# PEER block: nops between scattered adds, scatters paced in blocks of nine, four first-product banks, and 24 instead of 32 tokens by gathered rows

## The chip, the core and the metric

One core of a Trainium2 chip runs the whole kernel as one program. The time is device microseconds of one execution, the median of several; the engines are TensorE (PE; its weight loads are PEld), VectorE (DVE), ScalarE (ACT), GpSimd (POOL) and the DMA queues of SyncE (SP), ACT and POOL.

## The reference

One decoder layer over 512 tokens of width 1024 in float32: a projection, gated linear attention, sliding-window attention, an output projection, and then PEER, a layer of 16384 single-neuron experts. Only PEER is touched:

```
best, pos = lax.top_k(cand, 16)                  # 8 heads x 16 experts for each token
idx  = take_along_axis(cand_idx, pos);  gate = softmax(best)
u = expert_u[idx];  h = gelu(einsum('lkd,ld->lk', u, x))
out = einsum('lk,lkd->ld', gate * h, expert_v[idx])
```

A token needs 128 rows of U and of V, and the 512 tokens together need nearly all experts.

## The kernel before

The kernel computes PEER in two ways at once. For most tokens (TD = 352, columns TG = 160 to 511) it is **dense**: all 128 blocks of 128 experts are multiplied with all those tokens, and a matrix of gates (g, mostly zeros) picks what counts. For the first 160 tokens rows are **gathered**.

*Dense.* A first product (h_step, "U block") multiplies one block of U with the tokens: 24 matmuls of 352 columns (L202; 8 pieces of the width, three products of split float32 each), then ACT applies Gelu (L1334) into a ring, of which most is spilled to DRAM (hs) and loaded back later. A second product (v_step, "V block") multiplies gate times h (wr, w_a; split into wh and wl) with a block of V: again 24 matmuls (L1384), into eight banks that stay open for a phase. There are three phases: 92 U blocks and 92 V blocks, 20 and 20, 16 and 16; called U1, V1, U2, V2, U3, V3 here. Every block's weights (512 KB) come through SP's queue (raw), ACT rounds them (whi, L141) and DVE takes the difference (wlo, L151). The first products write to two PSUM banks in turn (M0, M1).

*The gates.* For tokens 160 to 383 (56 groups of four) DVE builds one-hot matrices (oh), PE multiplies them (gp, L1154, between the matmuls of U blocks), ACT copies them to gbuild, and SP writes them to DRAM (gd). For tokens 384 to 511 the gates (w3) are added into a zeroed DRAM array (g3) by 128 scatters on POOL, L1110, one for each pair of head and rank; a tiny store (memset of gap, L1109) stands ahead of each. Inside a head's 16 scatters no order is asked for; the first of a head waits until all of the head before have landed (after, L1120). Before each U block's pump some scatters are written into POOL's stream, so that all are out by block 88. The first V block needs gd, all of g3 and so the last head's landing: g_load loads both into gt, 32 times in all, the first two at block 89.

*Gathered rows.* The first 128 tokens, one per partition, take 128 row gathers on POOL (L1268, 1 MB each: U row and V row of one expert for each partition); tokens 128 to 159 are put four times beside each other (XR = 4 copies of XG = 32), which takes 32 more. For each, DVE multiplies U with x and sums (L1304), ACT makes the gated Gelu (L1305, L1306, tile misc), and DVE adds the V row (L1288). While the gates are being built ("early") these rows lie in two buffers named row; later in two pairs named rows.

*Order.* All engines run their own stream in program order. What stands where is planned while the program is written: pump() keeps running sums of what PE, DVE, POOL and the DMA queue would have used (pe, dve, pool, dma) and puts a step of the gather in when none is ahead of PE by more than SLACK; an early row is used three pumps after its issue at the earliest. What the planner did not fit in is done at once (flush, behind block 122 and so ahead of the last five blocks of V3).

Of the kernel before, what the change touches and what calls it, by code (L numbers as in the profile page):

```python
# [23 lines left out]
KB = 8  # L24
# [22 lines left out]
NRP = 11  # L47
# [6 lines left out]
GL = 3  # L54
XG = 32
# [6 lines left out]
CT = 32  # L62
NCK = TD // CT
NSC = 128 // CT
NGR = (TD - 128) // 4
CQ = CT // 4

# [6 lines left out]
def tile_block(ctx, tc, xT, wst, smalls, wgk2, keysT, uT, vv, uv_rows, out):  # L74
# [934 lines left out]
    gd = DR.tile([NB // 4, 128, NCK - NSC, 4 * CT], F32, name="gd")  # L1009
# [42 lines left out]
    def decode(t):  # L1052
        ij = R.tile([128, 2, 128], F32, name="ij", tag="ij", bufs=2)
        for sd in range(2):
            eq = eq_mult(t, sd)
            yield
            yield from tree(ij[:, sd], eq)
        gf = gate[:, t].rearrange("p h k -> p k h")
        if t == 0:
            nc.vector.scalar_tensor_tensor(eidx, ij[:, 0], 128.0, ij[:, 1], OP.mult, OP.add)  # L1060
            nc.vector.tensor_copy(wgt.rearrange("p (k h) -> p k h", h=8), gf)
            return
        if t == 3:
            nc.vector.tensor_copy(w3.rearrange("p (k h) -> p k h", h=8), gf)
            place(ij)
            return
        gk = R.tile([128, 128], F32, name="gkh", tag="gkh")
        nc.vector.tensor_copy(gk.rearrange("p (k h) -> p k h", h=8), gf)
        if t == 1:
            e1 = R.tile([128, 128], I32, name="e1")  # L1070
            nc.vector.scalar_tensor_tensor(e1, ij[:, 0], 128.0, ij[:, 1], OP.mult, OP.add)
            for r in range(XR):
                rs, n = slice(r * XG, (r + 1) * XG), min(XS, 128 - r * XS)
                nc.sync.dma_start(eid2[rs, 0:n], e1[0:XG, r * XS:r * XS + n])
                nc.sync.dma_start(wgt2[rs, 0:n], gk[0:XG, r * XS:r * XS + n])
# [10 lines left out]
    gap = XP.tile([1, 1], F32, name="gap")  # L1086
# [3 lines left out]
    def place(ij):  # L1090
        r4 = R.tile([128, 128], I32, name="r4")
        tk = R.tile([128, 4], I32, name="tk")
        nc.gpsimd.iota(tk[:, 0:1], pattern=[[0, 1]], base=0, channel_multiplier=1)
        nc.vector.tensor_scalar(tk[:, 1:2], tk[:, 0:1], 96, None, OP.bitwise_and)
# [10 lines left out]
        nc.vector.scalar_tensor_tensor(addr, f, 32.0 - 16384.0, a, OP.mult, OP.add)  # L1105

    def scatter(h, k):
        c = k * 8 + h
        nc.gpsimd.memset(gap, 0.0)  # L1109
# [8 lines left out]
        pool[0] += 2.1  # L1118
# [26 lines left out]
    def gmm(n):  # L1145
# [3 lines left out]
        if q == 0:  # L1149
            gbs[c] = Dn.tile([128, 128, CT], F32, name="gbuild", tag="gbuf", bufs=2)  # L1150
# [5 lines left out]
        if q == CQ - 1:  # L1156
            g = gbs.pop(c).rearrange("p (q i) t -> p q (i t)", i=4)

            def put(x):
                nc.sync.dma_start(gd[x:x + 4, :, c].rearrange("q j x -> j q x"), g[:, x:x + 4])  # L1160
                xfer(0.9)

            gout.extend([lambda x=x: put(x) for x in range(0, 32, 4)])

    def route():
# [76 lines left out]
    nc.gpsimd.memset(misc[:, 384:384 + 2 * XS], 0.0)  # L1242

    def gather():
# [8 lines left out]
        def issue(k):  # L1255
            nonlocal grp, n
            while n < min(n_, k + (3 if late[0] else 2)):
                for i in range(min(2 if late[0] else 1, n_ - n)):
# [19 lines left out]
        for k in range(n_ + 1):  # L1278
            if k:
                kind, s_ = slots[k - 1]  # L1280
# [19 lines left out]
            if k < n_:  # L1300
# [4 lines left out]
                nc.scalar.activation(hc, hc, AF.Gelu)  # L1305
                nc.scalar.activation(hc, hc, AF.Copy, scale=w_[0:m, s_:s_ + 1])  # L1306
# [8 lines left out]
    later = []  # L1315
# [87 lines left out]
    per = NGR / (N0 - LEAD - TAIL - 3) / KB  # L1403
    due = [0.0]

    def feed():
        due[0] += per
        while due[0] >= 1:
            due[0] -= 1
            next(r_, None)  # L1410


    def pump():
        for x in (dve, dma, pool):
            x[0] = max(x[0], pe[0] - SLACK)
        turn[0] += 1
# [46 lines left out]
    BANKS = ("S2", "S2", "PT", "O", "M2", "M3", "M0", "M1")  # L1463
    for ph, (b0, b1) in enumerate(PHASES):
        for b in range(b0, b1):
# [4 lines left out]
            h_step(b, feed if LEAD <= b < N0 - TAIL - 3 else None)  # L1470
# [144 lines left out]
```

## Time and profile before

| | |
|---|---|
| runs | 1807.66 us median of 3 (1807.25 to 1811.36) |
| profiled execution | 1808.49 us, its span 1806.6 us |
| busy share of PE, DVE, ACT, POOL | 94%, 73%, 42%, 43% |
| moved by DMA | 436.69 MB, 242 GB/s over the span |
| mean granted TensorE clock | 0.974 of full |

The busy shares are means over stages that have different limits: from 0 to 665 us the kernel computes attention, the projections and the routing scores; from 665 us the dense PEER runs. A stage is read from its own window, and a stall from the row of the engine that waits and of the one that released it.

### The profile page before, as it was taken

The page shows a single profiled execution, that of the slowest core. Times are in us where ns is not written, and L with a number is a line of the kernel's source. Part 1 is how long each engine was busy: PE and PEld are TensorE (multiplying, and loading weights), DVE is VectorE, ACT ScalarE, POOL GpSimd, SP SyncE. Part 2 cuts the span into 40 slices and gives each one's busy share as a digit, 9 for nine tenths or more (in the row PEclk, how much of TensorE's full clock was granted, in tenths as well). Part 3 has the DMA queues.
Part 4 walks back from the last instruction along what each step waited for, and adds up shares of the span by engine and source line. Part 5 has one row for each costly group of instructions (what it writes and reads, how often), then busy time and mean ns, then how long its engine had stood idle before and what let it go on. Part 6 is the DMA issues. An engine that isn't in the chain of part 4 may idle for free.

```text
span 1806.6 us, 26403 instructions
## 1 busy us (share of the span) xinstructions
PE 1690.4 (94%) x9812; PEld 1558.2 (86%) x9812; DVE 1321.8 (73%) x2491; ACT 760.0 (42%) x1360; POOL 782.1 (43%) x601
## 2 busy tenths in 40 slices
PE   7899999999997999999899897999999999999974
PEld 5676688987886889999899897999999999999973
DVE  7647714346246997996777754898898988998986
ACT  5445523335244234454454443444444444444431
POOL 3333444444544451788877782222221332332230
PEclk9999999999998999999999998999999999999986
DMA  4223442222243234699899999999999999998984
GB/s 158 79 70 94 145 136 81 70 82 71 93 143 136 84 107 140 195 271 274 261 281 283 276 288 331 377 402 403 404 394 402 381 357 385 378 402 354 373 339 172
DMA packets 161521, 436.69 MB, mean 242 GB/s; under 512 B 30720, under 2 KB 76160, under 8 KB 140528
## 3 DMA queue, kind: packets, MB, share of 16 engines
q1 hardware_dynamic: 114880, 254.53, 40.5%
q0 software_dynamic: 41472, 167.86, 26.2%
q10 hardware_dynamic: 5040, 12.62, 1.9%
q8 instruction: 77, 1.26, 0.3%
q14 instruction: 52, 0.43, 0.1%
HBM read 394.45 MB, written 40.47 MB: 241 GB/s over the span
## 4 chain that ended last, share of the span: by engine, by line
PE 61%; DVE 14%; DMA 11%; issue 5%; ACT 4%; POOL 3%; SPq 1%; POOLq 0%; DVEq 0%; ACTq 0%
PE mm L202 17%; PE oa L1384 16%; PE hp L202 13%; PE oacc L1384 5%; DMA rows<-in_uv_rows_dram,misc 5%; PE mm L219 4%; DVE wlo L151 2%; POOL g L1110 2%; DMA raw<-in_uT_dram 1%; DMA row<-in_uv_rows_dram,misc 1%; DVE accv L1288 1%; PE gp L1154 1%; DMA g<-w,addr 1%; ACT whi L141 1%; DMA gd<-gbuild 1%
## 5 line engine op out<-in xcount | busy, mean ns | idle before, releaser
L141 ACT CAST whi<-raw 128x1024 fp32r<-128x1024 f32 x349 | 362.9, 1043 | 129.1 <-DMA raw<-in_vv_dram 30.1
L1268 POOL DMA_INDIRECT rows<-in_uv_rows_dram,misc x128 | 187.9, 1468 | 490.1 <-DVE accv L1288 374.4
L202 PE MATMUL hp<-xh,whi 128*128 128x352 f32 x1024 | 340.3, 332 | 35.4 <-ACT hw L1334 29.2
L151 POOL TENSOR_TENSOR wlo<-raw,whi 128x1024 fp32r<-128x1024 f32 x99 | 244.5, 2474 | 240.2 <-ACT whi L141 235.3
L202 PE MATMUL hp<-xh,wlo 128*128 128x352 f32 x1024 | 334.6, 327 | 0.0
L202 PE MATMUL hp<-xl,whi 128*128 128x352 f32 x1024 | 333.2, 325 | 0.0
L151 DVE TENSOR_TENSOR wlo<-raw,whi 128x1024 fp32r<-128x1024 f32 x250 | 304.9, 1221 | 37.7 <-ACT whi L141 16.1
L1110 POOL DMA_INDIRECT g<-w,addr x128 | 246.1, 1922 | 102.3 <-issue 37.7
L1384 PE MATMUL oa<-wh,wlo 128*128 128x352 f32 x768 | 249.8, 325 | 33.0 <-DVE wlo L151 33.0
L1384 PE MATMUL oa<-wh,whi 128*128 128x352 f32 x768 | 249.6, 325 | 0.0
L1384 PE MATMUL oa<-wl,whi 128*128 128x352 f32 x768 | 249.5, 325 | 0.0
L202 PEld LDWEIGHTS hp<-xh,whi 128*128 128x128 f32 x1024 | 196.4, 192 | 39.5 <-ACT hw L1334 32.2
L202 PEld LDWEIGHTS hp<-xl,whi 128*128 128x128 f32 x1024 | 196.4, 192 | 0.0
L202 PEld LDWEIGHTS hp<-xh,wlo 128*128 128x128 f32 x1024 | 195.9, 191 | 0.0
L1305 ACT ACTIVATE misc<-misc 128x1 f32<-128x1 f32 x160 | 32.5, 203 | 353.1 <-DVE rows L1304 235.7
L1384 PEld LDWEIGHTS oa<-wh,wlo 128*128 128x128 f32 x768 | 145.8, 190 | 33.5 <-DVE wlo L151 33.5
L1384 PEld LDWEIGHTS oa<-wh,whi 128*128 128x128 f32 x768 | 146.4, 191 | 0.8 <-issue 0.8
L1384 PEld LDWEIGHTS oa<-wl,whi 128*128 128x128 f32 x768 | 145.9, 190 | 0.0
L1288 DVE SCALAR_TENSOR_TENSOR accv<-rows,misc,accv 128x1024 f32<-128x1024 f32 x96 | 123.1, 1282 | 13.4 <-ACT misc L1306 13.3
L1304 DVE SCALAR_TENSOR_TENSOR rows<-rows,xtok 128x1024 f32<-128x1024 f32 x96 | 117.3, 1222 | 10.5 <-DMA rows<-in_uv_rows_dram,misc 10.4
L202 PE MATMUL mm<-hhi,whi 128*128 128x512 f32 x264 | 107.2, 406 | 0.9 <-DVE gb L602 0.9
L202 PE MATMUL mm<-hhi,wlo 128*128 128x512 f32 x264 | 103.2, 391 | 0.0
(582 smaller groups left out, 3395.6 us busy)
## 6 DMA issues: line engine op xcount, KB each, us to landing
raw<-in_uT_dram SPq DMA_DIRECT2D x128, 512.0 KB, 5.5
raw<-in_vv_dram SPq DMA_DIRECT2D x128, 512.0 KB, 8.3
raw<-in_wst_dram SPq DMA_DIRECT2D x93, 512.0 KB, 3.5
gd<-gbuild SPq DMA_DIRECT2D x56, 256.0 KB, 6.5
gt<-gd SPq DMA_DIRECT2D x32, 448.0 KB, 7.8
hs<-hw ACTq DMA_DIRECT2D x35, 352.0 KB, 6.4
ring<-hs SPq DMA_DIRECT2D x35, 352.0 KB, 10.1
g<-zero SPq DMA_DIRECT2D x16, 512.0 KB, 5.4
```

What stands on the lines that cost most here:

```text
L141: nc.scalar.copy(hi, self.raw[u])
L151: self.lo_eng(u).tensor_tensor(lo, r, hi.bitcast(F32), OP.subtract)
L202: nc.tensor.matmul(ps[:, :n], a[:, kb, :], b[:, kb, c0:c0 + n], start=(kb == 0 and i == 0), stop=(kb == KB - 1 and i == 2))
L219: nc.tensor.matmul(banks[t], a[:, kb, t * 128:(t + 1) * 128], b[:, k, :], start=(first and k == 0 and i == 0), stop=(last and k == kk - 1 ...
L1110: i = nc.gpsimd.indirect_dma_start(out=g3, out_offset=bass.IndirectOffsetOnAxis(ap=addr[:, c:c + 1], axis=0), in_=w3[:, c:c + 1], in_offse ...
L1154: nc.tensor.matmul(p[:, k], o[:, 0, k], o[:, 1, k], start=True, stop=True)
L1268: nc.gpsimd.indirect_dma_start(out=rows[n][0:m, :], out_offset=None, in_=uv_rows, in_offset=bass.IndirectOffsetOnAxis(ap=ix[0:m, slots[n][ ...
L1288: nc.vector.scalar_tensor_tensor(a_, cur, h_[0:m, s_:s_ + 1], a_, OP.mult, OP.add)
L1304: nc.vector.scalar_tensor_tensor(cur, cur, 1.0, xs_[kind][0:m, :], OP.mult, OP.mult, accum_out=hc)
L1305: nc.scalar.activation(hc, hc, AF.Gelu)
L1384: nc.tensor.matmul(accs[c][:, 0:TD], v_[:, cs], a, start=(first and i == 0), stop=(last and i == 2))
```

## The change

1. The store ahead of each scatter becomes a nop, and scatters are written by a table: HD = (3, 2, 2, 3, 2, 2, 2, 0, 0) in nine U blocks, that is one head's 16 in seven blocks and none in two.
2. U blocks of the first phase use four banks in turn: two of every four go to the halves of S2.
3. XG is 24: five copies beside each other (120 partitions), XS = 26 gathers in place of 32; each gather fetches all 128 partitions. The dense part has TD = 360 tokens, 58 groups of gates, and its gate array is cut into 7 chunks of 32 tokens and small ones of 8 (CL), so that w_a multiplies in two pieces. The ring keeps one pair less (NRP 10).
4. The Gelu of an early row is held back (pend) and issued ahead of the next U block's Gelu (gates()). An early row is used when the planner's PE clock is LAND = 10 us past its issue; POOL may run 9 us ahead in the plan; a scatter counts 2.3 and a row 1.5 us of POOL.
5. The gates are done three blocks earlier; the writes of gd that remain are spread over the U blocks; the first two g_load are at block 88, on POOL's queue.

```
 def scatter(h, k):
-    nc.gpsimd.memset(gap, 0.0)
+    nc.gpsimd.nop()
     i = nc.gpsimd.indirect_dma_start(out=g3, ..., compute_op=OP.add).ins
-    pool[0] += 2.1
+    pool[0] += 2.3
+    xfer(0.33)
...
 def issue(k):
-    born[n] = turn[0]
     nc.gpsimd.indirect_dma_start(
-        out=rows[n][0:m, :], ...
+        out=rows[n], ...
-    pool[0] += 1.27
+    pool[0] += 1.5
+    born[n - 1] = max(pe[0], pool[0])
...
-    nc.scalar.activation(hc, hc, AF.Gelu)
-    nc.scalar.activation(hc, hc, AF.Copy, scale=w_[0:m, s_:s_ + 1])
+    pend.append((hc, w_[0:m, s_:s_ + 1]))
+    if late[0]:
+        gates()
...
 def h_step(b, each=None):
-    bank = PS.tile([128, 512], F32, name="hp", tag=f"M{b % 2}")
+    if b < N0 and b % 4 < 2:
+        if b % 2 == 0:
+            two[0] = PS.tile([128, 2, 512], F32, name="hp2", tag="S2")
+        bank = two[0][:, b % 2]
+    else:
+        bank = PS.tile([128, 512], F32, name="hp", tag=f"M{b % 2}")
...
+    gates()
     nc.scalar.activation(ring[p][:, b % 2], ps[:, :TD], AF.Gelu)
...
-def g_load(q):
-    nc.sync.dma_start(g[:, 0:NCK - NSC], gd[q])
+def g_load(q, eng=nc.sync):
+    eng.dma_start(g[:, 0:GO], gd[q])
...
 def w_a(p):
-    nc.vector.tensor_tensor(wr..., ring.pop(p)..., g, OP.mult)
+    for x0, x1, t0, t1, ct in PIECES:
+        nc.vector.tensor_tensor(wr[:, :, t0:t1]..., h[:, :, t0:t1]..., g[:, x0:x1]..., OP.mult)
...
 def feed():
-            next(r_, None)
+            if next(r_, 0) == 0:
+                per[0] = 0.5
+                if gout:
+                    gout.pop(0)()
...
 def pump():
-    if side and max(dve[0], dma[0], pool[0]) < pe[0] + SLACK:
-        if nxt and not late[0] and turn[0] < born[nxt[0]] + 3:
+    if side and max(dve[0], dma[0], pool[0] - (0 if late[0] else POOLQ)) < pe[0] + SLACK:
+        if nxt and not late[0] and pe[0] < born[nxt[0]] + LAND:
...
     if b == N0 - GL:
-        g_load(0)
-        g_load(1)
+        ...
+        g_load(0, nc.gpsimd)
+        g_load(1, nc.gpsimd)
-    k = round(len(scs) / max(N0 - GL - 1 - b, 1) + (b % 2 - 0.5) / 2)
+    k = HD[(b - b_s) % len(HD)]
```

What this does to the streams is seen at three places. POOL's stream at the end of the gates, before (gap is the tiny store, g_79 the array that is scattered into, rows the gathered rows):

```order
L1109 MEMSET gap 1x1
L1110 DMA g_79<-w_5483,addr 2097152x1
L1109 MEMSET gap 1x1
L1110 DMA g_79<-w_5483,addr 2097152x1
L1268 DMA rows<-in_uv_rows_dram,misc 128x2048 x128
```

The same place now (row is an early row, gt the gates for the second product; a nop is no row):

```order
L1120 DMA g_79<-w_5483,addr 2097152x1 x7
L1285 DMA row<-in_uv_rows_dram,misc 128x2048
L1120 DMA g_79<-w_5483,addr 2097152x1 x3
L1285 DMA row<-in_uv_rows_dram,misc 128x2048
L1120 DMA g_79<-w_5483,addr 2097152x1 x6
L1285 DMA rows<-in_uv_rows_dram,misc 128x2048 x4
L1377 DMA gt<-gd 128x928
L1378 DMA gt<-g_79 128x512
L1377 DMA gt<-gd 128x928
L1378 DMA gt<-g_79 128x512
L1285 DMA rows<-in_uv_rows_dram,misc 128x2048 x126
```

The stream has 24 early and 130 late rows, where it had 32 and 128; rows stand right behind the last scatter of heads 2, 3 (two), 4, 6 and 7 (two) of eight, where before one stood so, behind head 7; and four loads of gt stand between the fourth and the fifth late row.

ACT's stream in the middle of U1, before (misc is the gated Gelu of a gathered row, hw the Gelu of a U block, gbuild the copy of gates):

```order
L1305 ACTIVATE misc<-misc 128x1
L1306 ACTIVATE misc<-misc 128x1
L141 CAST whi_7609<-raw_7558 128x1024
L1155 COPY gbuild<-gp 128x4x128
L1334 ACTIVATE hw<-hp 128x352
```

And now:

```order
L149 CAST whi_7457<-raw_7408 128x1024
L1166 COPY gbuild<-gp 128x4x128
L1258 ACTIVATE misc<-misc 128x1
L1259 ACTIVATE misc<-misc 128x1
L1360 ACTIVATE hw<-hp 128x360
```

The two steps on misc moved behind the cast of the next weights and the copy of the gates; hw still stands behind them.

DVE's stream where the flush begins, before (wl belongs to the second product, wlo to the weights, accy sums the gathered V rows):

```order
L1288 SCALAR_TENSOR_TENSOR accy<-rows,misc,accy 128x1024
L1374 TENSOR_TENSOR wl<-wr,wh 128x704
L151 TENSOR_TENSOR wlo_15900<-raw_15830,whi_15866 128x1024
L1304 SCALAR_TENSOR_TENSOR rows,misc<-rows,xtk_14248 128x1024
L1288 SCALAR_TENSOR_TENSOR accy<-rows,misc,accy 128x1024
```

And now:

```order
L1307 SCALAR_TENSOR_TENSOR accy<-rows,misc,accy 120x1024
L1323 SCALAR_TENSOR_TENSOR rows,misc<-rows,xtk_14474 120x1024
L1402 TENSOR_TENSOR wl<-wr,wh 128x720
L159 TENSOR_TENSOR wlo_15949<-raw_15876,whi_15912 128x1024
L1307 SCALAR_TENSOR_TENSOR accy<-rows,misc,accy 120x1024
L1323 SCALAR_TENSOR_TENSOR rows,misc<-rows,xtk_14474 120x1024
```

From the last wlo shown to the next wr the pair of L1304 and L1288 stood 12 times; now nine rows are begun there (L1323), and the tenth L1307 ends a row begun ahead of the wlo.

## Rows read from the trace of the kernel before

**Rows 1.** Windows of U1, V1, flush: length, busy (count) PE/PEld/DVE/ACT/POOL, PE clock, DMA, GB/s

```profile
665.29:1114.05 448.76, 415.06 (x2664) 411.50 (x2662) 328.29 (x675) 204.22 (x314) 316.34 (x307) 0.97 0.85 256
1114.05:1470.89 356.84, 356.58 (x2208) 355.92 (x2208) 321.08 (x363) 155.34 (x256) 88.41 (x58) 0.99 0.99 388
...
1748.70:1781.65 32.95, 0.00 (x0) 0.00 (x0) 24.38 (x31) 5.57 (x20) 8.29 (x7) 0.55 0.88 315
```

**Rows 2.** PE's waits, 660 to 1120 us: total us, times, longest

```profile
PE hp L202 <- ACT hw L1334: 29.2, 11, 9.9
PE oacc L1384 <- ACT wh L1368: 4.0, 1, 4.0
```

**Rows 3.** Timeline of DVE and ACT around one late row, 978 to 982 us

```profile
978.39 1.23 DVE L1304 SCALAR_TENSOR_TENSOR row<-row,xtok 128x1024 f32<-128x1024 f32 x1 [7.51 <-DMA row<-in_uv_rows_dram,misc]
...
979.66 0.20 ACT L1305 ACTIVATE misc<-misc 128x1 f32<-128x1 f32 x1 [10.13 <-DVE row L1304]
...
981.86 0.49 ACT L1334 ACTIVATE hw<-hp 128x352 f32<-128x352 f32 x1
```

**Rows 4.** Line L1110, who waited for the scatters' landing: us, times

```profile
  POOL g L1110: 36.7, 7
```

**Rows 5.** Timeline of POOL: start us, us, instruction, idle before and releaser

```profile
722.23 2.45 POOL L1110 DMA_INDIRECT g<-w,addr  x1 [35.09 <-DVE addr L1105]
...
877.85 3.63 POOL L1110 DMA_INDIRECT g<-w,addr  x1 [0.27 <-issue]
...
966.98 1.55 POOL L1110 DMA_INDIRECT g<-w,addr  x1 [0.27 <-issue]
968.83 1.29 POOL L1268 DMA_INDIRECT row<-in_uv_rows_dram,misc  x1 [0.30 <-issue]
...
1088.26 1.55 POOL L1110 DMA_INDIRECT g<-w,addr  x1 [0.27 <-issue]
...
1090.11 1.55 POOL L1110 DMA_INDIRECT g<-w,addr  x1 [0.27 <-issue]
1091.97 1.88 POOL L1268 DMA_INDIRECT rows<-in_uv_rows_dram,misc  x1 [0.30 <-ACT whi L141]
```

**Rows 6.** Timeline of SP's queue and DVE at the end of U1

```profile
1070.22 13.33 SPq L1160 DMA_DIRECT2D gd<-gbuild  x8
...
1100.57 0.33 SPq L1351 DMA_DIRECT2D gt<-gd  x1
...
1112.24 0.89 DVE L1364 TENSOR_TENSOR wr<-ring,gt 128x704 f32<-128x704 f32 x1 [8.72 <-DMA gt<-g]
```

**Rows 7.** Chain of waits: start us, us, work and count

```profile
509.94 5.47 PE mm L202 x24
...
765.46 0.89 PE gp L1154 x8
766.35 4.28 PE hp L202 x27
```

**Rows 8.** Groups on POOL, 722 to 1092 us: busy us, mean ns, idle before and releasers

```profile
L1110 POOL DMA_INDIRECT g<-w,addr x128 | 246.1, 1922 | 102.3 <-issue 37.7 <-DVE addr L1105 35.1 <-DMA g<-w,addr 29.1
L1109 POOL MEMSET gap<- 1x1 f32 x127 | 61.3, 483 | 0.0
L1268 POOL DMA_INDIRECT row<-in_uv_rows_dram,misc x32 | 40.0, 1248 | 9.8 <-issue 7.6 <-DVE oh L1141 1.5 <-DVE wlo L151 0.6
```

**Rows 9.** Groups on DVE, V1 (1120 to 1456 us): busy us, mean ns, idle

```profile
L151 DVE TENSOR_TENSOR wlo<-raw,whi 128x1024 fp32r<-128x1024 f32 x87 | 106.3, 1221 | 7.3 <-ACT wh L1368 5.3 <-ACT whi L141 1.2 <-issue 0.8
...
L1364 DVE TENSOR_TENSOR wr<-ring,gt 128x704 f32<-128x704 f32 x43 | 38.2, 889 | 0.0
```

**Rows 10.** Timeline of DVE: first row of the flush, and first work behind it

```profile
1739.62 1.22 DVE L1304 SCALAR_TENSOR_TENSOR rows<-rows,xtk 128x1024 f32<-128x1024 f32 x1
...
1779.58 0.89 DVE L1364 TENSOR_TENSOR wr<-ring,gt 128x704 f32<-128x704 f32 x1
```

**Rows 11.** Timeline of DVE, its wait ahead of the last late rows

```profile
1091.75 1.23 DVE L151 TENSOR_TENSOR wlo<-raw,whi 128x1024 fp32r<-128x1024 f32 x1 [9.02 <-ACT whi L141]
```

More of the change, by code (lines that the diff above doesn't have):

```diff
@@ L46 @@
 N0 = 92
-NRP = 11
+NRP = 10
 NOO = 4
@@ L53 @@
 DUTY = 0.97
-GL = 3
-XG = 32
+LAND = 10.0
+POOLQ = 9.0
+GL = 4
+HD = (3, 2, 2, 3, 2, 2, 2, 0, 0)
+XG = 24
 XR = 128 // XG
@@ L61 @@
 TD = T - TG
-CT = 32
-NCK = TD // CT
-NSC = 128 // CT
+CT, CL = 32, 8
 NGR = (TD - 128) // 4
+NCT = (TD - 128 - CL) // CT
+GA, GB = NCT * 4 * CT, (1 + 128 // CL) * 4 * CL
+GO = GA + 4 * CL
+assert NCT * CT + CL == TD - 128
 CQ = CT // 4
+PIECES = [(0, GA, 0, NCT * CT, CT), (GA, GA + GB, NCT * CT, TD, CL)] if CL < CT else [(0, GA + GB, 0, TD, CT)]
 PHASES = [(0, N0), (N0, N0 + 20), (N0 + 20, NB)]
@@ L1066, in decode, with copy @@
             return
-        gk = R.tile([128, 128], F32, name="gkh", tag="gkh")
+        eg = R.tile([128, 2, 128], F32, name="eg", tag="eg")
+        gk = eg[:, 1]
         nc.vector.tensor_copy(gk.rearrange("p (k h) -> p k h", h=8), gf)
         if t == 1:
[L1070 to L1075, printed above, removed]
+            nc.vector.scalar_tensor_tensor(eg[:, 0].bitcast(I32), ij[:, 0], 128.0, ij[:, 1], OP.mult, OP.add)
+            def copy(r):
+                n = min(XS, 128 - r * XS)
+                nc.sync.dma_start(misc[r * XG:(r + 1) * XG, 384:384 + 2 * XS].rearrange("p (s k) -> p s k", s=2)[:, :, 0:n],
+                                  eg[0:XG, :, r * XS:r * XS + n])
+            gout.extend([lambda r=r: copy(r) for r in range(XR)])
         yield
@@ L1232, in route @@
             yield
-        while gout:
-            gout.pop(0)()
     late, early, used, acc2 = [False], [0], [-1], []
-    turn, nxt, born = [0], [], {}
+    nxt, born = [], {}
     sel = XP.tile([128, XG], F32, name="sel")
@@ L1242, in tile_block, with gates @@
     nc.gpsimd.memset(misc[:, 384:384 + 2 * XS], 0.0)
+    pend = []
+    def gates():
+        for h, w in pend:
+            nc.scalar.activation(h, h, AF.Gelu)
+            nc.scalar.activation(h, h, AF.Copy, scale=w)
+        pend.clear()
     def gather():
@@ L1265, in issue @@
                         early[0] = n + 1
-                    born[n] = turn[0]
-                    m, ix = use[slots[n][0]][0::3]
+                    ix = use[slots[n][0]][3]
                     nc.gpsimd.indirect_dma_start(
-                        out=rows[n][0:m, :], out_offset=None, in_=uv_rows,
-                        in_offset=bass.IndirectOffsetOnAxis(ap=ix[0:m, slots[n][1]:slots[n][1] + 1], axis=0))
+                        out=rows[n], out_offset=None, in_=uv_rows,
+                        in_offset=bass.IndirectOffsetOnAxis(ap=ix[:, slots[n][1]:slots[n][1] + 1], axis=0))
                     n += 1
-                    pool[0] += 1.27
+                    pool[0] += 1.5
+                    born[n - 1] = max(pe[0], pool[0])
                     xfer(2.54)
@@ L1314, in tile_block @@
     ring, gts, wrs, ws, accs = {}, {}, {}, {}, {}
-    later = []
+    later, two = [], [None]
     def get(kind, b):
@@ L1333, in h_step @@
                 ring[p] = Dn.tile([128, 2, TD], F32, name="ring", tag="ring", bufs=NRP)
+        gates()
         nc.scalar.activation(ring[p][:, b % 2], ps[:, :TD], AF.Gelu)
@@ L1402, in tile_block @@
     r_ = route()
-    per = NGR / (N0 - LEAD - TAIL - 3) / KB
+    per = [NGR / (N0 - LEAD - TAIL - 6) / KB]
     due = [0.0]
     def feed():
-        due[0] += per
+        due[0] += per[0]
         while due[0] >= 1:
             due[0] -= 1
-            next(r_, None)
+            if next(r_, 0) == 0:
+                per[0] = 0.5
+                if gout:
+                    gout.pop(0)()
     def pump():
@@ L1487, in tile_block @@
             if b == N0 - GL:
-                g_load(0)
-                g_load(1)
-            pool[0] = max(pool[0], pe[0] - SLACK)
-            k = round(len(scs) / max(N0 - GL - 1 - b, 1) + (b % 2 - 0.5) / 2)
-            for x in scs[:k]:
-                scatter(*x)
-            del scs[:k]
+                assert next(r_, 0) == 0
+                while gout:
+                    gout.pop(0)()
+                g_load(0, nc.gpsimd)
+                g_load(1, nc.gpsimd)
+            pool[0] = max(pool[0], pe[0] - SLACK)
+            if scs:
+                b_s = min(b_s, b)
+                k = HD[(b - b_s) % len(HD)]
+                for x in scs[:k]:
+                    scatter(*x)
+                del scs[:k]
             if b >= RS[-1]:
```

33 lines of the change are left out of this document (16 added, 17 removed).

## The prediction, made before the changed kernel ran

> **What bounds the kernel now.** I read the windows first. From 665 us the kernel is U1, V1 and two smaller pairs. In U1 PE is busy 415 of 449 us at a granted clock of 0.97, in V1 356.6 of 356.8, and in the flush not at all for 33 us [rows 1]. So two stretches have something to give: U1 and the flush. V1 and what follows are filled by PE, with the DMA engines at 0.99, and there more PE work is more time.
>
> The waits of PE say what holds U1: 29.2 us for ACT's Gelu, and 4.0 for the first wh of V1 [rows 2]. That Gelu takes 0.49 us and is not itself the cause. In the timeline DVE waits 7.51 us for a gathered row, the step on misc behind it keeps ACT idle for 10.13, and hw stands behind both; PE has only two banks and stops [rows 3]. Why are the rows late? POOL's timeline answers: from the first scatter at 722.23 to the first late row at 1091.97 POOL never waits for a free buffer, only for a head's landing, 36.7 us in seven waits [rows 4, 5]. POOL is the bound of U1, and PE's stalls pass POOL's lateness on. The chain at its end: the eight gd writes, issued at once, hold SP's queue 13.3 us; the loads of gt go out at 1100.57, wr starts at 1112.24, PE at 1114.05 [rows 1, 6].
>
> **The change part by part.**
>
> *Wider dense part.* 24 matmuls of 352 columns take 24 x 4.28/27 = 3.80 us, and one of 512 columns 5.47/24 = 0.228 against 0.1585 us [rows 7]. That is 0.434 ns a column, so eight columns more cost 24 x 8 x 0.434 ns = 0.083 us a block: 7.7 us in the 92 blocks of U1, 7.7 in V1, and 6.0 in the 72 others. Two more groups of gates are 2 x 0.89 = 1.8 us [rows 7]. In V1 and later nothing hides it: +13.7 us on the path. In U1 it only moves PE's own limit, worked out next.
>
> *U1, PE's limit.* 92 x 3.887 + 58 x 0.89 = 409 us, so PE could end U1 at 665.3 + 409 = 1074. Before, its need was 400 of 449 us.
>
> *U1, POOL's limit.* From 722.2 to 1092.0 are 369.7 us. Off go 36.7 for landings and 32 rows of 1.25 + 0.30 = 1.55 us (busy plus the issue gap), 49.6 [rows 4, 5, 8]; what is left, 283.4, is 2.21 us for each of 128 scatters. After the change: 128 x 2.21 = 283.4; 24 early rows are 37.2; six more rows than before stand right behind a head's last scatter and run inside the landing, 6 x 1.55 = 9.3, so the landings cost 27.4. The sum is 348.0, and POOL is through at 1070.2 in place of 1092.0. From there to V1's first matmul I keep the measured 22.1 us (1091.97 to 1114.05): four late rows, the last head's landing, the loads of gt, wr, wh. V1 starts at 1092.3, that is 21.8 us earlier, and 18 us behind PE's own limit, which covers what remains of row stalls in U1.
>
> The loads of gt now stand in POOL's stream: queued behind them is the fifth late row, which would wait for a buffer anyway. SP's weight loads no longer wait behind them.
>
> *The nop.* The store looks like 61.3 us of POOL [rows 8], but it runs beside the end of the scatter. A scatter with a store behind it starts the next one 1.85 us later (1088.26 to 1090.11), and a scatter with a row right behind it and no store starts that one 1.85 us later too (966.98 to 968.83) [rows 5]. So I take the swap at nothing. The trace shows no nop and no two scatters back to back. Ends: the whole gap of 0.30 us won or lost per scatter, 38 us on POOL either way, where a win of more than 18 us is cut off by PE's limit.
>
> *Four banks, held-back Gelu, LAND.* They take no work away. With four banks PE can go two U blocks (7.8 us) further past a blocked hw; of the eleven waits in the listed 29.2 us the longest, 9.9, stood behind SP's burst, and the other ten have 1.9 at the mean [rows 2, 6]. I cost them at nothing because POOL sets the end of U1; they matter only if POOL gets faster. The spread gd writes likewise: PE had waited 9.9 us for that burst, but inside the time that POOL needed.
>
> *wr in two pieces.* On DVE 1024 elements take 1221 ns and 704 take 889 [rows 9], so an instruction has 159 ns beside 1.04 ns an element. Two pieces of together 720 take 1064 ns: with the longer wl +0.19 us a pair, 8.8 us in V1. DVE has 356.8 - 321.1 = 36 us free there [rows 1]; hidden. If that cover is gone, up to +9.
>
> *Late rows and flush.* 130 late rows in place of 128, of which nine, not 12, are left to the flush. The flush took 1779.58 - 1739.62 = 39.96 us for 12, 3.33 each [rows 10]; three fewer are -10.0 us of PE's 33 us wait [rows 1]. The five rows more that run beside PE bring 5 x 1.05 MB, at V1's 388 GB/s 13.5 us [rows 1], and PE's blocks are longer by 13.7 there: just covered. If it isn't, they come back as wait, up to +13.
>
> *Sum,* against the profiled execution's 1808.49 us (span 1806.6 and 1.9 around it): -21.8 + 7.7 + 6.0 - 10.0 = -18.1, so 1790.4. The median is 0.8 below that execution, so 1790.
>
> **The rivals.**
>
> *POOL gets out of the way.* The last scatters took 1.55 us, while DVE waited 9.02 us for ACT; the mean is 1.92, and one at 877.85 took 3.63 [rows 5, 8, 11]. With DVE less often in the way, or nops that let scatters close up, POOL may end before PE. Then V1 starts at PE's limit, 1074.5 plus 2 us for wr and wh: -37.6 + 13.7 - 10.0 = -33.9, 1774. For it: eight fewer rows on DVE; against: two more groups of one-hots and the shorter U1 leave DVE as dense as before.
>
> *POOL is as late as ever.* V1 starts at 1114 again, because scatters get longer by what rows and landings save. 21.8 us is 0.17 us a scatter. Then +13.7 - 10.0 = +3.7, 1811. For it: lengths of 1.55 to 3.63 us, the short ones beside an idle DVE, and in a U1 without stalls DVE is idle less. Against: DVE's work in U1 falls by eight rows of 2.5 us, 328 - 20 + 3 = 311 of 427 us, 73% as before [rows 1].
>
> The Trainium skill (SBUF — State Buffer, section SBUF: two separate sides) says that DVE and GpSimd share a port pair that one of them holds for a whole instruction while the other stands still. By that rule this rival follows wherever DVE gets denser; the trace agrees as to the short ones (1.55 us beside an idle DVE, 1.92 at the mean), and at equal density the rule leaves the scatter at its 2.21.
>
> *Nops cost what stores hid.* The place is POOL between two scatters: if a nop is not run beside the scatter's end but takes an issue gap of its own, 0.30 us, POOL ends 38.4 us later, at 1108.6, and V1 starts at 1130.7: +16.7 + 13.7 - 10.0 = +20.4, 1828, slower. It decides from 0.14 us a nop on (18 us, where the whole gain is gone). For it: no row shows a nop, and every instruction on POOL that was listed starts 0.27 to 0.30 us behind the one ahead; against: the two equal distances of 1.85 us.
>
> **How the numbers follow.** Less than 0.3% (5.4 us) is what a measurement of this kernel can't tell from no change. The forecast (about 1780 to 1802, with 1790 its centre): 0.55. POOL out of the way (1774): 0.17. As late as ever (1811, some of it with a part of the gain): 0.18. Nops that cost (1828, or less with a part of it, or DVE and DMA in V1 uncovered on top of it): 0.10. Faster by over 0.3%, that is below 1802: the first two and a little of the third, 0.74. Within: 0.15. Slower: 0.11. The range of 8 in 10 leaves out half of the best case and the worst: 1775 to 1812.
>
> **What would show it.** Right: POOL's first late row near 1070 us and V1's first matmul near 1092; scatters at a mean of 2.2 us from start to start outside the landings; PE's waits for hw in U1 down by half or more, the 9.9 gone; V1 at 364 to 366 us; PE's wait in the flush near 23 us. Wrong: V1 starting at 1080 or before (POOL was no bound any more), or at 1110 or later with longer distances between scatters (the nop or DVE); rows of wlo waits inside V1 (DVE had no room); a flush wait of 30 us (the late rows were not covered).

## The result and the profile after

The changed kernel takes 1819.25 us (median of 9 runs, 1817.05 to 1826.35) against 1807.17 for the kernel before on the same chip (9 runs): a ratio of 1.0068, 95% interval 1.0045 to 1.0090. It is slower, where 1790 was forecast. The profiled execution took 1819.01 us with a span of 1817.1.

Windows of the changed kernel (columns as in [rows 1]): U1, V1, flush.

```profile
668.16:1112.30 444.14, 426.17 (x2682) 419.25 (x2680) 315.44 (x662) 208.44 (x300) 288.31 (x176) 1.00 0.82 244
1112.30:1478.25 365.95, 365.44 (x2208) 365.06 (x2208) 333.86 (x417) 159.27 (x267) 84.52 (x62) 1.00 0.99 388
1765.57:1790.45 24.88, 0.01 (x2) 0.00 (x1) 18.03 (x23) 4.09 (x14) 5.13 (x4) 0.57 0.88 305
```

| From the first matmul of ... | before | after | difference | predicted |
|---|---|---|---|---|
| start to V1 | 1114.05 | 1112.30 | -1.8 | -21.8 |
| V1 to U2 | 359.1 | 366.0 | +6.8 | +7.7 |
| U2 to V3 (56 blocks) | 222.7 | 235.1 | +12.4 | +4.7 |
| V3 to the end, flush in it | 110.7 | 103.8 | -6.9 | -8.7 |
| span | 1806.6 | 1817.1 | +10.5 | -18.1 |

So 20 of the 28.6 us that the forecast was off lie ahead of V1: 17 in U1, and 3 ahead of it, since its first matmul is at 668.16, not 665.05. The stalls of U1 behind late rows [rows 2] are gone. In their place stand the waits below (total us, times, longest): many short ones.

```profile
PE hp L210 <- ACT hw L1360: 12.3, 16, 1.8
PE hp L210 <- ACT ring L1360: 3.5, 5, 1.2
PE hp L210 <- issue: 1.1, 2, 0.6
```

There are 23 of them, one at every fourth U block; 16 last 0.56 us, the others 0.23 to 1.80, and they add up to 16.9 us. Timeline of PE, then of ACT, at one of them:

```profile
688.84 0.32 PE L210 MATMUL hp<-xh,wlo 128*128 128x360 f32 x1
689.72 0.43 PE L210 MATMUL hp<-xh,whi 128*128 128x360 f32 x1 [0.56 <-ACT ring L1360]
...
689.20 0.47 ACT L1360 ACTIVATE ring<-hp 128x360 f32<-128x360 f32 x1 [2.59 <-PE hp L210]
```

The matmul at 688.84 is the last of a block, the Gelu at 689.20 reads that same block, and the next block starts only behind it: 0.88 us from start to start where matmuls inside a block are 0.166 apart, a loss of 0.71 us, and 16.4 us over the 23 such blocks of U1 if all were like this one. A block should not wait for the Gelu of the block right ahead of it, which has another bank. The change to the program suggests why it does: two blocks of four share one tile, S2, and the wait falls on the second of them. The dependency is kept by tile, not by bank; the experiments with separate tiles show it.

POOL was no longer what U1 waited for: ahead of V1 PE waits only 1.1 us for wh, so it is itself through as late as 1111.2. POOL's groups (as [rows 8]), and its timeline at the end of U1 (as [rows 5]):

```profile
L1120 POOL DMA_INDIRECT g<-w,addr x128 | 231.0, 1805 | 89.8 <-issue 42.9 <-DVE addr L1115 38.6 <-DMA g<-w,addr 7.7
L1285 POOL DMA_INDIRECT row<-in_uv_rows_dram,misc x24 | 32.3, 1347 | 33.3 <-DVE accv L1307 28.4 <-issue 3.3 <-DVE wlo L159 0.9
```

```profile
1076.83 1.54 POOL L1120 DMA_INDIRECT g<-w,addr  x1 [0.30 <-DMA gd<-gbuild]
1079.73 0.99 POOL L1285 DMA_INDIRECT rows<-in_uv_rows_dram,misc  x1 [1.35 <-issue]
...
1094.32 0.97 POOL L1285 DMA_INDIRECT rows<-in_uv_rows_dram,misc  x1 [12.32 <-DMA raw<-in_uT_dram]
...
1101.40 0.59 POOL L1377 DMA_DIRECT2D gt<-gd  x1 [4.87 <-DVE accv L1307]
```

Landings cost 7.7 us, not 29.1 [rows 8], but rows now wait 28.4 us for accv, that is for DVE to be through with an earlier row. The first late row goes out at 1079.73 (before 1091.97), and the third and fourth only 13 us behind the second.

Behind V1 the largest new loss is at the start of U3. Timeline of DVE, ACT and PE there:

```profile
1643.52 1.23 DVE L1323 SCALAR_TENSOR_TENSOR rows<-rows,xtok 128x1024 f32<-128x1024 f32 x1 [2.18 <-DMA rows<-in_uv_rows_dram,misc]
...
1646.16 0.81 ACT L1466 COPY ev<-oa 128x360 f32<-128x360 f32 x2
...
1647.03 0.67 PE L210 MATMUL hp<-xh,whi 128*128 128x360 f32 x1 [8.84 <-ACT ev L1466]
```

A late row lands late, its gates and the next cast follow on ACT, ev stands behind them, and PE waits 8.84 us where it waited 3.4 before.

### The profile page after: what moved, and what is told of

It is laid out like the page before. It is cut to its first block, busy times and chain, and to the rows that moved or that the text cites. A ratio compares the mean times of both kernels' runs of the same rounds, so it can differ in the third digit from the quotient of the medians.

```text
span 1817.1 us, 26366 instructions
## 1 busy us (share of the span) xinstructions
PE 1721.5 (95%) x9828; PEld 1586.5 (87%) x9828; DVE 1321.7 (73%) x2547; ACT 767.5 (42%) x1350; POOL 751.1 (41%) x472
## 4 chain that ended last, share of the span: by engine, by line
PE 73%; DVE 10%; DMA 8%; ACT 4%; issue 3%; POOL 1%; SPq 0%; POOLq 0%; DVEq 0%; ACTq 0%
PE hp L210 21%; PE oa L1412 18%; PE mm L210 16%; PE oacc L1412 6%; DMA rows<-in_uv_rows_dram,misc 6%; PE mm L227 4%; PE gp L1165 3%; POOL rows L1285 1%; DMA raw<-in_vv_dram 1%; DVE wlo L159 1%; PE sc L954 1%; DVE accv L1307 1%; DMA gt<-gd 0%; DVE stt L434 0%; DMA xt<-in_xT_dram 0%
## 5 line engine op out<-in xcount | busy, mean ns | idle before, releaser
L210 PE MATMUL hp<-xh,whi 128*128 128x360 f32 x1024 | 344.5, 336 | 25.7 <-ACT hw L1360 12.3
L210 PE MATMUL hp<-xl,whi 128*128 128x360 f32 x1024 | 337.2, 329 | 0.0
L210 PE MATMUL hp<-xh,wlo 128*128 128x360 f32 x1024 | 336.6, 329 | 0.0
L1412 PE MATMUL oa<-wh,wlo 128*128 128x360 f32 x768 | 252.7, 329 | 24.9 <-DVE wlo L159 24.9
L1120 POOL DMA_INDIRECT g<-w,addr x128 | 231.0, 1805 | 89.8 <-issue 42.9
L1412 PE MATMUL oa<-wh,whi 128*128 128x360 f32 x768 | 252.6, 329 | 0.0
L1412 PE MATMUL oa<-wl,whi 128*128 128x360 f32 x768 | 252.0, 328 | 0.0
L1307 DVE SCALAR_TENSOR_TENSOR accv<-rows,misc,accv 128x1024 f32<-128x1024 f32 x104 | 133.2, 1281 | 11.8 <-ACT misc L1259 11.5
L1323 DVE SCALAR_TENSOR_TENSOR rows<-rows,xtok 128x1024 f32<-128x1024 f32 x104 | 126.9, 1220 | 9.2 <-DMA rows<-in_uv_rows_dram,misc 9.1
L1258 ACT ACTIVATE misc<-misc 128x1 f32<-128x1 f32 (+1 forms) x154 | 31.5, 204 | 215.0 <-DVE rows L1323 213.3
```

The source lines that it names most:

```text
L210: nc.tensor.matmul(ps[:, :n], a[:, kb, :], b[:, kb, c0:c0 + n], start=(kb == 0 and i == 0), stop=(kb == KB - 1 and i == 2))
L1120: i = nc.gpsimd.indirect_dma_start(out=g3, out_offset=bass.IndirectOffsetOnAxis(ap=addr[:, c:c + 1], axis=0), in_=w3[:, c:c + 1], in_offse ...
L1258: nc.scalar.activation(h, h, AF.Gelu)
L1307: nc.vector.scalar_tensor_tensor(a_, cur, h_[0:m, s_:s_ + 1], a_, OP.mult, OP.add)
L1323: nc.vector.scalar_tensor_tensor(cur, cur, 1.0, xs_[kind][0:m, :], OP.mult, OP.mult, accum_out=hc)
L1412: nc.tensor.matmul(accs[c][:, 0:TD], v_[:, cs], a, start=(first and i == 0), stop=(last and i == 2))
```

## The experiments

Each run's profiled execution gives its stages. Between executions of one kernel the time varies by half a per cent and more, so whether a kernel is faster is read from the ratio to the kernel before on the same chip.

**Two banks in place of four.**

```diff
-        if b < N0 and b % 4 < 2:
-            ... two[0] = PS.tile([128, 2, 512], F32, name="hp2", tag="S2") ... bank = two[0][:, b % 2]
-        else: ...
+        bank = PS.tile([128, 512], F32, name="hp", tag=f"M{b % 2}")
```

> The changed kernel with two first-product banks as before (M0 and M1 in turn), everything else as changed. Theory A (two blocks that share one tile S2: the second one's first matmul waits for the Gelu of the first one, 0.72 us more than a plain step, 23 times in U1, 16.6 us): these waits are gone, and V1 starts near 1112.3 - 15 = 1097 if nothing else stands there; 1804 us in all. Rival B (the four banks are what removed PE's row stalls in U1): the eleven stalls of the kernel before come back, up to 29 us, V1 starts at 1112 to 1125; 1819 to 1832 us. Rival C (the loads of gt, issued at 1101.40 on POOL behind late rows and the fourth early accv, set V1's start): PE's waits in U1 go but V1 still starts at 1110 to 1112, PE waits some 14 us for wh there; 1817 to 1819 us.

Measured: ratio 0.9996 (0.9967 to 1.0024), 1810.36 us; V1 starts at 1099.02. PE's waits from 660 to 1100 us, and the timeline of POOL and DVE:

```profile
PE oacc L1407 <- ACT wh L1391: 6.3, 1, 6.3
PE hp L210 <- ACT hw L1355: 3.4, 3, 1.9
```

```profile
1071.19 1.65 POOL L1285 DMA_INDIRECT rows<-in_uv_rows_dram,misc  x1 [0.30 <-issue]
...
1083.75 0.59 POOL L1372 DMA_DIRECT2D gt<-gd  x1 [5.94 <-DVE accv L1307]
...
1096.74 0.62 DVE L1386 TENSOR_TENSOR wr<-ring,gt 128x448 f32<-128x448 f32 x1 [10.59 <-DMA gt<-gd]
```

Theory A holds: the waits are gone, V1 starts 13.3 us earlier, and the other stages keep their lengths (366.8, 234.3 and 103.0 us). Rival B is refuted: with two banks the row stalls stay away. POOL's first late row is at 1071.19; 1070.2 was predicted. Rival C holds for the rest: PE is through at 1092.8 and waits 6.3 us for wh, which waits for gt.

**Four banks that are four tiles.** The first kernel takes them from block 0 on, the second only from block 24 on.

```diff
+        bank = PS.tile([128, 512], F32, name="hp", tag=("S2", "PT", "M0", "M1")[b % 4] if b < N0 else f"M{b % 2}")
# the second kernel:  ... [b % 4] if 24 <= b < N0 else f"M{b % 2}")
```

> The changed kernel with four first-product banks that are four tiles of one bank each (one in S2's place, one in PT's, M0, M1) in place of one tile of two banks and two of one. Theory A (the shared tile): no wait at every fourth block any more, V1 starts near 1097, 1803 us, and not later than the kernel with two banks. Rival C (gt's loads set V1's start): as the kernel before the edit within 2 us, V1 at 1110 to 1112, 1817 to 1819 us, with PE's wait moved to V1's first matmul. A third, D (PE waits for Gelu because a bank needs its Gelu anyway, however the tiles are cut): the 0.56 us waits stay, 1819 us.

> The changed kernel (360 columns) with two banks up to block 23 and four tiles of one bank each from block 24 on, where S2 and PT have no other user. Theory A (the pair in one tile was the fault, and two banks are enough with the other edits): as with two banks, V1 at 1097 to 1101, 1810 us within 0.3%, no waits for hw above 1 us. If four banks that are really apart take more out of U1: two banks still had 3.5 us of waits for hw, so V1 at most 4 us earlier, and gt's loads may keep it at 1099. If V1 starts at 1109 as with four tiles from block 0 on (7.4 us for the top-k in PT at block 1): the order of the banks, not the top-k, was the fault there.

From block 0 on: ratio 1.0024 (0.9995 to 1.0053), V1 at 1109.5. The beat is gone, which refutes D, but PE lost 11 us elsewhere, by a fault of this edit: block 1 wanted PT while the last scores lay in it, waiting for the top-k.

```profile
PE hp L210 <- DVE w L944: 7.4, 1, 7.4
PE oacc L1407 <- ACT wh L1391: 6.2, 1, 6.2
PE hp L210 <- DVE wlo L159: 3.6, 1, 3.6
```

From block 24 on: V1 at 1094.9 (in an execution 11 us below the median), with 0.4 us of PE's waits in U1 and 7.0 for wh at V1. The time is 1.0024 (1.0003 to 1.0045) of before. So four separate banks take some 3 us of waits out of U1, which the time does not show; two are enough.

**The pair alone, in the kernel before.**

```diff
-        bank = PS.tile([128, 512], F32, name="hp", tag=f"M{b % 2}")
+        if b < N0 and b % 4 < 2: ... two[0] = PS.tile([128, 2, 512], F32, name="hp2", tag="S2") ...
```

> The kernel before with the change's four first-product banks (two blocks of four in one tile S2, M0 and M1 for the others) and nothing else. Theory A (the second block of the pair waits for the first one's Gelu, but POOL sets U1's end here, at 1092 for the first late row): waits of 0.56 us at every fourth block, some 16 us in all, while the stalls for late rows (29.2 us) shrink by about as much; V1 within 4 us of 1114, 1807 us within 0.3%. If the pair's waits come on top of the stalls: V1 at 1126 to 1131, 1820 to 1824 us. If four banks take the stalls out and the pair's waits are little: PE is through early and waits for wh, V1 still near 1114, with PE's waits for hw below 10 us.

Measured: 1.0036 (1.0009 to 1.0063), V1 at 1114.6, the first late row at 1092.90 (1091.97 before).

```profile
PE hp L202 <- ACT hw L1339: 23.7, 17, 4.8
PE oacc L1389 <- ACT wh L1373: 4.6, 1, 4.6
PE hp L202 <- ACT ring L1339: 3.9, 6, 1.4
```

The beat is there (0.55 us at 667.45, 683.54, 716.58 and so on), PE's waits in U1 add up to 31.0 us in all where they were 29.7, so the stalls behind rows are shorter by about as much as the beat adds, and V1 starts where it did. Where POOL ends U1, the pair costs little in U1 (451.8 us, 449.0 before); once POOL is quicker, it costs what the first experiment shows. The ratio leaves out 1: the median is some 6 us above before, and this profile, of an execution 11 us below the median, does not show where.

**Widths.** In the kernel before, U blocks 92 to 127 take turns. This kernel gives only the times of matmuls, not the layer's result.

```diff
+PROBE = ((352, 160, 0), (352, 152, 0), (360, 152, 8), (360, 144, 8), (368, 144, 16),
+         (368, 136, 16), (376, 136, 24), (384, 128, 32), (356, 156, 4))
+        n, c0, o = PROBE[(b - N0) % 9] if b >= N0 else (TD, TG, 0)
+        ps = proj(w, XN, n=n, c0=c0, bank=bank, each=each)
```

> The kernel before, with the first products of its last 36 U blocks at other widths and first columns, four blocks of each: 352 columns from 160, 352 from 152, 360 from 152 (the change's), 360 from 144, 368 from 144, 368 from 136, 376 from 136, 384 from 128, 356 from 156. Gelu reads 352 of them; in the second, fourth and sixth these are other tokens' columns. Start to start of matmuls. By the prediction's 0.434 ns a column: 352 0.159 us, 356 0.161, 360 0.1625, 368 0.166, 376 0.169, 384 0.173, whatever the first column. By steps of 16 columns (seen: 0.159 at 352, 0.166 at 360): 356, 360 and 368 all 0.166, 376 and 384 both 0.1725, whatever the first column. By the first column (a start that is no multiple of 16 columns costs 3 ns): 352 from 152 0.162, 360 from 144 0.1625, 360 from 152 0.166, 368 from 144 0.166, 368 from 136 0.169.

Timeline of PE: first and 24th matmul of four blocks (368 columns from 144, 356 from 156, 352 from 160, 352 from 152).

```profile
1484.59 0.32 PE L204 MATMUL hp<-xh,whi 128*128 128x368 f32 x1
...
1488.43 0.33 PE L204 MATMUL hp<-xh,wlo 128*128 128x368 f32 x1
...
1501.03 0.33 PE L204 MATMUL hp<-xh,whi 128*128 128x356 f32 x1
...
1504.85 0.33 PE L204 MATMUL hp<-xh,wlo 128*128 128x356 f32 x1
1505.02 0.32 PE L204 MATMUL hp<-xh,whi 128*128 128x352 f32 x1
...
1508.66 0.32 PE L204 MATMUL hp<-xh,wlo 128*128 128x352 f32 x1
1508.82 0.33 PE L204 MATMUL hp<-xh,whi 128*128 128x352 f32 x1
...
1512.55 0.32 PE L204 MATMUL hp<-xh,wlo 128*128 128x352 f32 x1
```

The distance of the two by 23 gives 167.0, 166.1, 158.3 and 162.2 ns. Medians over four blocks: 352 159.6 (from 152: 162.0), 356 166.1, 360 166.5 (from 144: 166.1), 368 167.0 (from 136: 167.6), 376 173.0, 384 174.1. In U, then, the medians rise in steps of 16 columns, about 7 ns each, whatever the first column; single blocks of 356 and 360 columns also took 163.5 to 164 ns, and one of 360 took 171.3. At 352 the start off the multiple of 16 has a median 2.4 ns higher, but single blocks overlap (158.3 to 163.0 and 160.0 to 162.2). V does not show the step: 160.1, 164.6 and 168.2 ns at 352, 360 and 368 columns in the kernels with these widths. The Trainium skill (TensorE: Matmul & The Clock Gate, section Back-to-back issue gap) has the gap of a matmul by itself grow evenly with the columns; for the stream of matmuls in U these runs measure otherwise.

**The nop alone,** in the kernel before.

```diff
-        nc.gpsimd.memset(gap, 0.0)
+        nc.gpsimd.nop()
```

> The kernel before with a nop in place of the store ahead of each scatter, and nothing else. POOL sets U1's end there, so its price shows whole. By the prediction (the store runs beside the end of the scatter, swap at nothing): scatters still 1.85 us apart, first late row near 1092, V1 near 1114, 1807 us within 0.3%. By the rival of nops that cost 0.30 us: 38 us later, 1845 us. If nops let scatters close up by the whole gap: 38 us of POOL won, V1 at PE's limit near 1095, 1788 us. A fourth, E (the store is an access of POOL to its memory port beside DVE, and scatters behind it are longer): scatters at a mean of 1.80 us in place of 1.92, 15 us of POOL won, V1 near 1099, 1793 us.

Measured: 1.0018 (0.9997 to 1.0039). POOL's timeline, two scatters with a nop between them and a row behind the second without one, 1.85 and 1.84 us apart, as with a store [rows 5]:

```profile
1092.78 1.54 POOL L1110 DMA_INDIRECT g<-w,addr  x1 [0.30 <-DMA raw<-in_uT_dram]
1094.63 1.54 POOL L1110 DMA_INDIRECT g<-w,addr  x1 [0.30 <-issue]
1096.47 1.74 POOL L1268 DMA_INDIRECT rows<-in_uv_rows_dram,misc  x1 [0.31 <-issue]
```

Scatters take 1888 ns at the mean (1922 with stores, but 1886 and 1882 in the kernels of the pair and of the widths, which have stores too). The first late row is at 1096.47 and V1 starts at 1118.97, both some 5 us late; in this execution early rows took 1476 ns for 1248, and landings 41.0 us for 36.7. The time shows no gain and no loss that can be told, as predicted; its interval allows a loss of up to 0.4%.

**Gates at once,** with two banks.

```diff
-                if late[0]:
-                    gates()
+                gates()
```

> The changed kernel with two banks, and with the gates of an early row (the two ACT operations on misc) issued at once again, not held back until the next Gelu of a U block. If held-back gates are what took PE's row stalls out of U1 (29.2 us before, 3.5 in the changed kernel with two banks): ACT waits again for a gathered row with the Gelu of hw behind it, PE's waits for hw rise to 15 to 30 us, V1 starts at 1105 to 1120, 1817 to 1830 us. If it is the waiting for a row's landing by planned time (LAND) and the blocks of scatters that did it: PE's waits for hw stay below 8 us, V1 at 1099 to 1103, 1810 us within 0.3%.

Measured: 1.0006 (0.9985 to 1.0027), waits for hw 10.3 us in 7 (3.4 in 3 held back), V1 at 1103.7. Between the two answers: holding back saves 7 us of stalls, which the time does not show, and is not what took most of the 29.2 away. What did is not separated: with scatters spread evenly (below) 14.7 us of these waits come back, and LAND has no run of its own.

**Three kernels on rows and width.** The first has four tiles from block 0 on, the others two banks.

```diff
-XG = 24 ... CT, CL = 32, 8
+XG = 32 ... CT, CL = 32, 32        # 352 columns
+XG = 16 ... CT, CL = 32, 16        # 368 columns
# even scatters, 360 columns:
-                k = HD[(b - b_s) % len(HD)]
+                k = round(len(scs) / max(N0 - GL - 1 - b, 1) + (b % 2 - 0.5) / 2)
```

> The changed kernel with four separate first-product banks and with the width undone: 32 tokens of tile two by row gathers, 352 dense columns, 128 late and 32 early rows. Matmuls go back from 0.166 to 0.159 us, which is 14.8 us in U1, 9.9 in V1 and 8 in the other 72 blocks; three more rows in the flush are +10 us. If PE sets U1's end: V1 starts at 1097 - 15 - 1.8 = 1080, and the time is 1080 + 692.5 = 1772 to 1776 us. If POOL and the loads of gt behind it set it: eight more early rows of 1.55 us put the last scatter 12 us later, V1 at 1112 to 1124, 1804 to 1817 us.

> The changed kernel with two banks, and with the scatters spread over the U blocks as before (by what is left, rounded, alternating) in place of heads in seven blocks of nine. If the blocks are what made POOL faster (rows and other work in the two blocks without scatters hide the landings: 18.4 us in 6 waits, 36.7 in 7 before): landing waits rise to 30 to 40 us, the last scatter comes 12 to 20 us after 1069, V1 starts at 1110 to 1118, 1822 to 1829 us. If it is the eight rows less on POOL and the early rows' pacing (POOL ahead of the plan is allowed for 9 us): landings rise, but V1 starts at 1099 to 1104, 1810 us within 0.3%.

> The changed kernel with two banks and 16 tokens of tile two by row gathers: 368 dense columns, 144 rows in place of 154 of which 24 are early. By the steps seen (360 columns 0.166 us, 368 0.167): 164 blocks x 24 x 1 ns = 4 us more PE, ten late rows less, so that the flush's nine rows are gone: its wait goes from 24.5 to under 5 us, 1790 us. By 0.434 ns a column: 24 x 8 x 0.434 ns = 0.083 us a block, +13.7 us, less the flush: 1799 us. If late rows are not what the flush waits for: the wait stays above 20 us, 1815 us.

| Kernel | early, late rows | V1 starts | V1 to span's end | PE's wait in the flush | ratio (interval) |
|---|---|---|---|---|---|
| before, 352 | 32, 128 | 1114.1 | 692.5 | 33.0 | 1 |
| two banks, 360 | 24, 130 | 1099.0 | 704.1 | 24.5 | 0.9996 (0.9967 to 1.0024) |
| 352 again, four tiles | 24, 136 | 1103.6 | 719.6 | 59.0 | 1.0101 (1.0056 to 1.0146) |
| even scatters, 360 | 31, 123 | 1122.9 | 677.0 | 6.6 | 0.9946 (0.9920 to 0.9973) |
| 368 | 27, 117 | 1100.3 | 684.6 | none | 0.9886 (0.9853 to 0.9919) |

Waits of PE with even scatters:

```profile
PE hp L210 <- ACT hw L1355: 14.7, 6, 7.2
PE oacc L1407 <- ACT wh L1391: 11.0, 1, 11.0
PE oa L1407 <- DVE wlo L159: 6.6, 1, 6.6
```

With 352 columns both answers missed, with the four-tile kernel's waits at U1's start in it (7.6 us for the top-k). I had 32 early rows in mind; the planner put 24 into U1, so eight more were late, and V1 to the end grew by 27.1 us over the kernel before: 3.4 us a row. With even scatters the landings came as the first answer had them (33.6 us in nine waits), but both missed the time: V1 starts 24 us later, and the kernel is faster, since seven more rows fit into U1 and V1 to the end is 27.1 us shorter, 3.9 us a row. U2 to V3 falls from 234.3 to 223.6 us, 8.7 of it in V2, and the wait for ev from 3.0 to 1.0: the loss there goes with late rows as well. 368 columns gave U at 167 ns, no flush and 1787.13 us, near the answer by steps, but in part by luck: V has no steps, and V1 took 377.1 us for 366.8, while the planner put three more rows into U1 than the 24 assumed.

**Where gt's load comes from.** On the 368-column kernel: the first four late rows issued behind the loads of gt, and, by itself, the loads on SP's queue.

```diff
+            if late[0] and not go[0]:        # issue(): hold late rows
+                held[:] = [lambda: issue(k)]
+                return
...
                 g_load(1, nc.gpsimd)
+                go[0] = True                 # then issue what was held
# the other kernel: g_load(0) and g_load(1) on nc.sync
```

> The kernel with 368 columns and two banks (1787 us), with the first four late rows issued behind the loads of gt in POOL's stream, not ahead of them. There gt was issued at 1083.77 and wr started at 1098.30, 14.5 us later, behind four rows of 1 MB issued at 1071.62 to 1075.54; PE waited 8.3 us for wh. If those rows are what delays gt (four of 2.7 us at 388 GB/s are 10.8 us): gt lands 5 to 7 us after its issue, PE's wait at V1 falls below 2 us, V1 starts near 1093, 1780 us. If it is the weights' loads or the length of the strided read of gd: V1 stays at 1099 to 1101, 1787 us within 0.3%. If the late rows then miss their time in V1: V1 starts sooner, but the stretch behind it is longer by as much.

> The kernel with 368 columns and two banks, with the first two loads of gt on SP's queue as before, not POOL's. If the queue is of no account (they wait for the last early row's accv either way, and no late row is kept back by them): V1 at 1099 to 1102, 1787 us within 0.3%. If they now hold up SP's weight loads behind them, as the prediction had it: raw for V1 comes later by the wait of 7.3 us, PE waits for whi or wlo inside the first V blocks by 5 to 10 us, 1792 to 1797 us. If POOL's software queue was what made gt slow (14.5 us): gt lands sooner, V1 near 1093, 1780 us.

Rows behind: 1780.03 us (1774.38 to 1785.06, 6 runs), ratio 0.9860 (0.9832 to 0.9888), better than both kernels of this case. POOL's and DVE's timeline:

```profile
1083.20 0.59 POOL L1376 DMA_DIRECT2D gt<-gd  x1 [13.34 <-DMA raw<-in_vv_dram]
...
1085.78 1.00 POOL L1289 DMA_INDIRECT rows<-in_uv_rows_dram,misc  x1 [0.30 <-issue]
...
1086.95 0.63 DVE L1390 TENSOR_TENSOR wr<-ring,gt 128x448 f32<-128x448 f32 x1 [1.39 <-DMA gt<-gd]
```

From gt's issue to wr are 3.8 us, not 14.5, and V1 starts at 1092.1 (1100.3): on POOL's queue, four rows of 1 MB ahead of it were the delay. V1 is then 382.8 us long, not 377.1, but the stages behind it are shorter, so from V1 to the end it is 685.8 us, not 684.6. Its interval overlaps that of the 368-column kernel, so this last step's own gain is shown by the traces (spans 1777.9 and 1784.9) and not by the ratios. By SP: 0.9887 (0.9851 to 0.9923), V1 at 1095.4 with PE still waiting 6.6 us for wh. Timeline of SP, DVE and ACT:

```profile
1079.46 0.33 SPq L1372 DMA_DIRECT2D gt<-gd  x1
...
1087.86 0.63 DVE L1386 TENSOR_TENSOR wr<-ring,gt 128x448 f32<-128x448 f32 x1 [5.71 <-DMA gt<-gd]
...
1093.28 1.04 ACT L149 CAST whi<-raw 128x1024 fp32r<-128x1024 f32 x1 [11.93 <-DMA raw<-in_vv_dram]
...
1094.60 0.79 ACT L1391 CAST wh<-wr 128x736 fp32r<-128x736 f32 x1
```

From gt's issue to wr are 8.4 us here, 6 less than by POOL behind the same four rows, but raw, now issued behind gt, comes late, and wh stands behind its cast on ACT. So the queue changes which load is late, gt or the weights; the time does not tell them apart. That SP's weight loads would wait behind gt is what the prediction had.

## Why the prediction was wrong, step by step

- **Four banks "at nothing".** This step failed, and it was the largest. It rested on POOL's end of U1 and on 18 us of cover behind PE's own limit. The pair in one tile was a wait of its own, and the cover was not there (below): 16.9 us of waits, 13.3 us of V1's start, 0.7% of the time (1.0068 with it, 0.9996 without). That two blocks share one tile was there to be read in the change.
- **POOL's limit (1070.2).** Near where the pair does not interfere, 1071.19, but with some luck: the first scatter came 6.7 us later than taken (728.88), and landings cost 18.4 us in place of 27.4. Scatters kept their length (1918 ns at the mean). With the pair, PE's lateness came back on POOL through DVE and the rows' buffers: rows waited 28.4 us for accv, 1.1 without it.
- **PE's limit (1074), the cover for that sum.** Too low by some 18 us: PE is through at 1092.8 with two banks, no earlier than the 1092.3 forecast for V1. The sum took 92 blocks at 3.887 us; at the measured 0.1658 us a matmul they take 3.98 (+8.5), U1 starts 4.4 us later in that execution, and 3.4 us of waits remain; what is left of the 18, some 2 us, is in small pieces. Of the late start about 3 us come with the change: in each of the six kernels of 360 columns PE waits 2.3 to 2.9 us for qb, the load of the keys, ahead of the routing scores, with 352 columns at most 1.25. Why that load is late is open.
- **The width, 0.083 us a block.** In V1 right: +6.8 us, 7.7 predicted. In U a mis-sized term: a step of 16 columns for 8, 0.16 us a block. [Rows 7] held 352 and 512 columns only, and a line through both hides steps.
- **The 22.1 us from the first late row to V1.** 27.8 with two banks. Before, four late rows went out ahead of gt's loads too; what is new is that the loads are issued 12.6 us behind the first late row, not 8.6, as POOL waits 5.94 us for accv ahead of them. From there to wr are 13.0 us (11.7), and from wr to V1 2.3 (1.8). The last experiment shows what was overlooked, at 368 columns: 10.7 us of this stretch are a delay that goes away when the rows stand behind the loads, and V1 then starts 8.2 us sooner.
- **Late rows "just covered".** Failed by about 5 us: U2 to V3 are 7.7 us over the forecast, of which the step of 16 columns takes up to 36 x 0.08 = 2.8 in the U blocks; the longer wait for ev at the start of U3 is 5.5. The prediction counted 130 late rows in place of 128 and compared means; all eight rows saved were early ones, hidden in U1. The flush itself came as forecast: 24.88 us, near 23.
- **The nop at nothing** and **wr in two pieces hidden:** right as far as the time can tell; 1.0018, and no wait for wr inside V1.
- **Rivals.** "POOL out of the way" had the mechanism, PE as what ends U1, but its price rested on PE's limit of 1074. "As late as ever" had V1's start nearly right (1114, measured 1112.3) for a reason that is refuted: scatters were not longer but 1805 ns, and 1918 with two banks, against 1922. So the shared port of the Trainium skill (SBUF — State Buffer, section SBUF: two separate sides) did not make scatters longer here; whether it has a part in their mean of 1.9 us, no run tests.

## What to carry to other kernels

Two buffers in one tile are one buffer to whoever keeps the dependencies: ask what a new buffer shares with another before you cost it at nothing. Where a resource fills the tail of a kernel, here rows of 1 MB beside PE, the count of units that fall into it is worth more than where a stage starts: at 3.4 to 3.9 us a row, seven rows outweighed a V1 that starts 24 us later. And a width is priced at the sizes used, not by a line between two others.

## What the runs showed of the hardware that was not expected

The steps of 16 columns in U (356 columns cost what 368 do, 166 and 167 ns) and their absence in V. Why V differs is open. The Trainium skill (Perfetto Trace Analysis, section Matmuls) wants independent matmul groups to rotate through different PSUM banks; here two banks left 3.4 us of waits in U1 and four separate ones 0.4, and the time did not tell them apart.
